# A hybrid decoder layer: attention and the down projection tied to the written instruction order, and four PSUM banks swapped in the second half

## The chip, the cores and the metric

The kernel runs on one core of one Trainium2 chip. The core has a matrix engine (TensorE, PE in the profile, with its weight loads as PEld), three engines for elementwise work (VectorE: DVE, ScalarE: ACT, GpSimd: POOL) and SyncE (SP), which issues all DMAs of this kernel. Each engine works through a list of instructions of its own, in the order of that list, and engines wait for each other through semaphores. The metric is the device time of one execution in microseconds (us).

## The reference

One layer of a decoder trunk over 2048 positions and 1024 channels, in float32. Two parts of it matter here, the forgetting attention (8 heads of 64) and the last product of the channel MLP:

```python
def forgetting_attention(q, k, v, f_pre):
    F = jnp.cumsum(jax.nn.log_sigmoid(f_pre.astype(jnp.float32)), axis=-1)
...
        logits = (jnp.einsum('bhtd,bhsd->bhts', qb, kb).astype(jnp.float32) * scale
                  + F[:, :, lo:hi, None] - F[:, :, None, :hi])
...
        p = jax.nn.softmax(logits, axis=-1)
        outs.append(jnp.einsum('bhts,bhsd->bhtd', p.astype(v.dtype), vb))

def conv_ffn(h, w_up, w_conv, b_conv, w_down):
...
    return (jax.nn.silu(a) * gv) @ w_down
```

Around them stand a norm, one combined input projection, an mLSTM and a gating unit, the output projection, the up projection and a causal convolution.

## The kernel before

The kernel is written with a tile framework. The program text names, for each instruction, its engine and its tiles; the framework allots buffers, sets the semaphores, and, with its scheduling turned on (line 1797), puts the instructions of each engine into an order of its own, from a simulated timeline. So the order in which the code writes two independent instructions of an engine is not the order in which the chip runs them.

The stages follow each other: projections and mLSTM, attention, output projection, up projection with convolution, down projection. Products of two float32 operands are made of three TensorE products of "hi" and "lo" halves (mm3, lines 53 to 56): ScalarE makes the hi half by a cast, VectorE the lo half by a subtraction.

**Attention** (lines 190 to 290). For each head h there are four blocks tb of 512 queries, each of four rows of 128 queries. `scores` handles a row in one or two parts of up to 1024 keys: TensorE makes the scores in a double-bank PSUM tile `sp` (two of them; lines 206 and 210), VectorE adds the bias, stores the tile L and keeps the row's extreme (line 212). For tb 0 and 1 a row has one part, of 128 to 512 and of 640 to 1024 keys; for tb 2 and 3 a part of 1024 keys and a second part of 128 to 512 and of 640 to 1024. `exps` (line 220) then makes a row's exponentials on ScalarE, one instruction for a part (line 223), and GpSimd scales L by the row's sum (lines 225 to 228). `exps` is called when the generator is resumed for the following part, so in the written order it stands just ahead of the next part's scores. `finish` takes a finished block in units j of 128 keys: up to four transposes on TensorE into a PSUM tile `tp` (three of them; line 259), a cast on ScalarE (262), a subtraction on VectorE (263), and, three units later, two products with the values (245 and 246) into the one bank `op`, which ScalarE copies out at the end of a block (250). `phase` (line 269) writes the two streams into one: the scores of one block with the units of the block before it. After part n of n_sc it writes units until (n + 1)(n_fin - 5) / n_sc are done, n_fin being 4, 8, 12 or 16 for a block tb of 0 to 3; the last five units, and all four of tb 0, stand behind the last part. While attention runs, `load_w` (line 309) also loads and splits the weights of the output projection.

**Down projection** (class Down, lines 486 to 636). The product of the activations with w_down is made by a seven-product scheme (Winograd's form of Strassen's), for each half H of the positions: products p in the order 1, 2, 7, 6, 5, 4, 3, each in 11 steps k of 12 matmuls, four banks at a time. `load` starts a step's DMAs five steps ahead. `prep` makes a step's operands three steps ahead: sums on VectorE (lines 1523 to 1539; one for products 5, 4 and 3, two for product 7, three for product 6), then for two operands a cast on ScalarE (1544) and a subtraction on VectorE (1545), into 12 tiles `wsp`, four for a step. `mm` issues the step's matmuls. `post` queues the evictions of a finished product in the list `later`, from which three are written behind each step (lines 1764 to 1766), in the next product's first three steps: 12 VectorE instructions for products 2, 5 and 4, four for product 7, 16 for product 6, 8 for product 3, and four ScalarE copies for product 1. The main loop, lines 1714 to 1769, writes for each step the loads, the `prep` of three steps on, the `mm`, then the evictions.

PSUM has eight banks; the down projection uses them as two sets of four, db0 and db1. Line 1555 counts the products that take a new set, and products alternate between the sets; product 3 adds into the banks of product 5 and isn't counted. So the six new sets of one half leave the count even, and product 1 of the second half takes the set that product 3 of the first half has just filled.

## Time and profile before

| what | value |
|---|---|
| median of 3 runs | 2715.94 us (2714.63 to 2721.72) |
| time of the profiled execution | 2716.23 us |
| its span, first to last instruction | 2714.5 us |
| PE busy | 2588.1 us |
| PEld busy | 2132.3 us |
| DVE busy | 1997.7 us |
| ACT busy | 1268.5 us |
| POOL busy | 412.0 us |
| mean granted TensorE clock | 0.984 |

The span is divided about so: projections and mLSTM to 719 us, where the first scores run; attention to 1192 us; output projection; up projection to 2232 us; down projection to the end. A line of a group names the source line, the engine, the operation, output and inputs, their shape and count, then the busy time, the mean of one in ns, and the idle time of the engine ahead of it with what ended it. A line of the timeline has the start, the length, the instruction, a count where equal ones are merged, and in brackets the idle time before it.

### The profile page before, as it was taken

Reading aid. Unit: us, or ns where it says so; the run is one execution under the profiler, and the core shown is the slowest. Engines: PE = TensorE matmul, PEld = TensorE weight load, DVE = VectorE, ACT = ScalarE, POOL = GpSimd, SP = SyncE. Lnnn points to the kernel's source line nnn. Section 1 sums busy time; section 2 is a strip of 40 time slices with the busy share of each in tenths; the row PEclk is TensorE's granted clock in tenths of the full one; section 3 lists DMA queues with packets and bytes.
Section 4 is the critical chain, followed back from the end, with each engine's and each line's share of the span. In section 5 each row is a group of like instructions: output and inputs, shape, how many; then the busy total and the mean of one; then the engine's idle time right before and its main releaser. Section 6 shows DMA issues by size and latency. Waiting matters only on the chain.

```text
span 2714.5 us, 36970 instructions
## 1 busy us (share of the span) xinstructions
PE 2588.1 (95%) x12761; PEld 2132.3 (79%) x12761; DVE 1997.7 (74%) x3460; ACT 1268.5 (47%) x2425; POOL 412.0 (15%) x550
## 2 busy tenths in 40 slices
PE   6999999999989999989989999999999999899899
PEld 5887878888768787877868888888888887678677
DVE  7546556574478888846679888888888877887886
ACT  4323342332368878834455444444444444334333
POOL 4012210122246656610000000000000000000000
PEclk8999999999999999999999999999999999999999
DMA  7626454334554535147632222264222248266523
GB/s 245 184 79 183 136 169 142 98 98 125 167 156 111 143 105 175 48 142 250 252 93 78 86 87 84 86 239 141 81 82 86 79 139 302 81 217 225 182 74 113
DMA packets 297812, 377.52 MB, mean 139 GB/s; under 512 B 31246, under 2 KB 189804, under 8 KB 295576
## 3 DMA queue, kind: packets, MB, share of 16 engines
q1 hardware_dynamic: 297624, 375.16, 43.5%
q8 instruction: 100, 1.64, 0.3%
q14 instruction: 88, 0.72, 0.1%
HBM read 274.34 MB, written 100.74 MB: 138 GB/s over the span
## 4 chain that ended last, share of the span: by engine, by line
PE 64%; DVE 9%; DMA 8%; issue 2%; ACT 1%; POOL 1%; SPq 1%; DVEq 0%; ACTq 0%; POOLq 0%
PE ub L55 10%; PE ub L54 10%; PE ub L56 10%; PE sp L206 4%; PE tp L259 3%; PE db L55 3%; PE db L56 3%; PE db L54 3%; PE acc L54 3%; PE acc L56 2%; PE acc L55 2%; PE op L246 2%; PE op L245 2%; DVE wspl L1545 2%; DMA ld<-y_d 2%
## 5 line engine op out<-in xcount | busy, mean ns | idle before, releaser
L54 PE MATMUL acc<-wh,hh 128*128 128x512 f32 (+2 forms) x768 | 284.6, 373 | 1.8 <-DVE vhl L783 1.0
L55 PE MATMUL db<-wspl,wsph 128*128 128x512 f32 x616 | 247.8, 402 | 31.5 <-DVE wspl L1545 31.4
L55 PE MATMUL acc<-wl,hh 128*128 128x512 f32 (+2 forms) x768 | 275.6, 361 | 0.3 <-DVE wl L625 0.3
L54 PE MATMUL ub<-T,wsph 128*128 128x512 f32 x704 | 273.1, 390 | 2.4 <-ACT T L1239 2.1
L55 PE MATMUL ub<-T,wsph 128*128 128x512 f32 x704 | 274.2, 390 | 0.6 <-DVE T L1240 0.6
L56 PE MATMUL ub<-T,wspl 128*128 128x512 f32 x704 | 272.9, 389 | 0.0
L56 PE MATMUL acc<-wh,hl 128*128 128x512 f32 (+2 forms) x768 | 271.9, 361 | 0.4 <-DVE hl L595 0.4
L56 PE MATMUL db<-wsph,wspl 128*128 128x512 f32 x616 | 243.7, 396 | 0.0
L263 DVE TENSOR_TENSOR plo<-tp,phi 128x512 fp32r<-128x512 f32 (+1 forms) x320 | 188.6, 606 | 57.7 <-ACT phi L262 55.8
L54 PE MATMUL ub<-B,wsph 128*128 128x512 f32 x528 | 207.5, 393 | 8.0 <-ACT s L1440 4.0
L55 PE MATMUL ub<-B,wsph 128*128 128x512 f32 x528 | 207.3, 393 | 0.0
L56 PE MATMUL ub<-B,wspl 128*128 128x512 f32 x528 | 207.0, 392 | 0.0
L1413 ACT CAST wsph<-S 128x512 fp32r<-128x512 f32 x176 | 109.2, 622 | 200.5 <-PE ub L55 153.6
L262 ACT CAST phi<-tp 128x512 fp32r<-128x512 f32 (+1 forms) x320 | 161.5, 520 | 83.6 <-PE tp L259 81.3
L1544 ACT CAST wsph<-act 128x512 fp32r<-128x512 f32 x132 | 82.3, 623 | 222.1 <-PE db L55 211.8
L223 ACT ACTIVATE L<-L,nm 128x1024 f32<-128x1024 f32 (+2 forms) x192 | 172.7, 903 | 17.2 <-DVE nm L212 15.5
L259 PE MATMUL tp<-ident,L 128*128 128x128 f32 x1088 | 174.1, 277 | 4.9 <-DVE plo L263 2.9
L206 PE MATMUL sp<-kk,q 128*128 128x512 f32 (+3 forms) x640 | 163.4, 373 | 14.2 <-DVE nm L212 7.9
L55 PEld LDWEIGHTS db<-wspl,wsph 128*128 128x128 f32 x616 | 117.7, 191 | 70.4 <-DVE wspl L1545 46.3
L54 PE MATMUL db<-wsph 128*128 128x512 f32 x616 | 168.7, 393 | 3.1 <-ACT wsph L1544 2.6
L228 POOL TENSOR_SCALAR L<-L,rs 128x1024 f32<-128x1024 f32 (+2 forms) x192 | 166.4, 876 | 11.7
L54 PEld LDWEIGHTS acc<-wh,hh 128*128 128x128 f32 x768 | 146.5, 191 | 21.3 <-DVE vhl L783 1.1
(344 smaller groups left out, 6050.8 us busy)
## 6 DMA issues: line engine op xcount, KB each, us to landing
w<-in_w_up_dram SPq DMA_DIRECT2D x88, 512.0 KB
wd<-in_w_down_dram SPq DMA_DIRECT2D x176, 256.0 KB
wa<-in_w_ada_dram SPq DMA_DIRECT2D x96, 256.0 KB
act_d<-yc SPq DMA_DIRECT2D x44, 512.0 KB
act<-act_d SPq DMA_DIRECT2D x44, 512.0 KB
wr<-in_w_in_dram SPq DMA_DIRECT2D x68, 256.0 KB
q<-q_d SPq DMA_DIRECT2D x128, 128.0 KB
hc_d<-hl SPq DMA_DIRECT2D x28, 512.0 KB
```

Of the source, the lines that this page charges most:

```text
L54: T.matmul(ps, lh, rh, start=start, stop=False, skip_group_check=resume)
L55: T.matmul(ps, lh, rl, start=False, stop=False, skip_group_check=resume)
L56: T.matmul(ps, ll, rh, start=False, stop=stop, skip_group_check=resume)
L206: T.matmul(sp[:, b : b + bw], q2[n][:, qs], kk[:, s0 + b : s0 + b + bw], start=n == 0, stop=n == 1 and not last)
L223: A.activation(L[c], L[c], AF.Exp, bias=nm[:, n - 1 : n], scale=-1.0, accum_out=rs[:, c : c + 1])
L228: G.tensor_scalar(t, t, rs[:, 0:1], 1.0, op0=ALU.mult, op1=ALU.mult)
L245: T.matmul(op[:, c0:], vv[:, j, :], hi[:, c0:], start=(j == 0), stop=False)
L259: T.transpose(tp[:, i * P : (i + 1) * P], rows[i][j // 8][:, (j % 8) * P : (j % 8 + 1) * P], ident)
L262: A.copy(hi[:, c0:], tp[:, c0:])
L263: V.tensor_tensor(lo[:, c0:], tp[:, c0:], hi[:, c0:].bitcast(F32), op=ALU.subtract)
L1413: A.copy(hi, src)
L1544: A.copy(hi, v)
```

## The change

`keep_in_program_order` takes an instruction and ties it behind the instruction that the code wrote just before it for the same engine: the scheduler may no longer move it ahead of that one. It sets the order of issue only and adds no wait for the end of the other. The change calls it O and wraps every TensorE, VectorE, ScalarE and GpSimd instruction of `scores`, `exps` and `finish`, and every VectorE and ScalarE instruction of Down. The matmuls of Down, all DMAs, and `load_split` stay free.

The second part moves one line: the count of bank sets goes up for product 3 too. Each half then counts seven, and the second half begins with the other set, so that its product 1 doesn't take the banks of the first half's product 3.

```diff
+    O = tc.keep_in_program_order
...
-                        T.matmul(
+                        O(T.matmul(
                             sp[:, b : b + bw], q2[n][:, qs], kk[:, s0 + b : s0 + b + bw], start=n == 0, stop=n == 1 and not last
-                        )
+                        ))
...
-                V.tensor_tensor_reduce(
+                O(V.tensor_tensor_reduce(
...
-                    A.activation(L[c], L[c], AF.Exp, bias=nm[:, n - 1 : n], scale=-1.0, accum_out=rs[:, c : c + 1])
+                    O(A.activation(L[c], L[c], AF.Exp, bias=nm[:, n - 1 : n], scale=-1.0, accum_out=rs[:, c : c + 1]))
...
-                    G.tensor_scalar(t, t, rs[:, 0:1], 1.0, op0=ALU.mult, op1=ALU.mult)
+                    O(G.tensor_scalar(t, t, rs[:, 0:1], 1.0, op0=ALU.mult, op1=ALU.mult))
...
-            T.matmul(op[:, c0:], vv[:, j, :], hi[:, c0:], start=(j == 0), stop=False)
+            O(T.matmul(op[:, c0:], vv[:, j, :], hi[:, c0:], start=(j == 0), stop=False))
...
-            A.copy(hi[:, c0:], tp[:, c0:])
-            V.tensor_tensor(lo[:, c0:], tp[:, c0:], hi[:, c0:].bitcast(F32), op=ALU.subtract)
+            O(A.copy(hi[:, c0:], tp[:, c0:]))
+            O(V.tensor_tensor(lo[:, c0:], tp[:, c0:], hi[:, c0:].bitcast(F32), op=ALU.subtract))
...
-                A.copy(hi, v)
-                V.tensor_tensor(lo, v, hi.bitcast(F32), op=ALU.subtract)
+                O(A.copy(hi, v))
+                O(V.tensor_tensor(lo, v, hi.bitcast(F32), op=ALU.subtract))
...
             if k == 0:
+                n_bank[0] += 1
                 if more:
                     self.ps[3] = self.ps[5]
                 else:
-                    n_bank[0] += 1
```

The sums of `prep` and all evictions of Down (lines 1523 to 1539 and 1579 to 1635) are wrapped in the same way.

## The prediction

> **What bounds the kernel now.** I read the page first, then the windows by stage, then the timeline and the groups by form inside the two stages that the change touches.

> ```profile
> span 2714.5 us, 36970 instructions
> ...
> PE 2588.1 (95%) x12761; PEld 2132.3 (79%) x12761; DVE 1997.7 (74%) x3460; ACT 1268.5 (47%) x2425; POOL 412.0 (15%) x550
> ```

> ```profile
> core 0: us, PE busy (x) PEld busy (x) DVE busy (x) ACT busy (x) POOL busy (x), PEclk, DMA share, GB/s
> ...
> 914.23:965.75 51.52, 49.40 (x313) 41.10 (x313) 43.68 (x89) 42.60 (x93) 30.97 (x48) 1.00 0.42 124
> ...
> 2300.10:2380.90 80.80, 67.88 (x265) 51.97 (x265) 69.68 (x115) 25.13 (x45) 0.00 (x0) 0.94 0.32 108
> 2380.90:2477.10 96.20, 92.16 (x397) 73.53 (x395) 80.00 (x132) 38.24 (x68) 0.00 (x0) 1.00 0.73 254
> ...
> 2537.30:2617.20 79.90, 65.42 (x266) 49.55 (x265) 69.97 (x116) 25.12 (x45) 0.00 (x0) 0.98 0.29 97
> 2617.20:2707.80 90.60, 90.54 (x397) 73.96 (x395) 71.65 (x118) 35.36 (x62) 0.00 (x0) 1.00 0.35 116
> ```

> The page says TensorE. By stage it is less plain. The first window is one whole head of attention: 51.52 us, with TensorE, VectorE and ScalarE all at 83% or more. The other four are the down projection, for each half products 7 and 6, then 5, 4 and 3. In 7 and 6 TensorE is idle by some 13 us.

> What a head costs TensorE alone comes from the distance of starts:

> ```profile
> 939.31 0.60 PE L259 MATMUL tp<-ident,L 128*128 128x128 f32 x4
> ...
> 940.21 0.60 PE L259 MATMUL tp<-ident,L 128*128 128x128 f32 x4
> ...
> 941.12 0.60 PE L259 MATMUL tp<-ident,L 128*128 128x128 f32 x4
> ```

> ```profile
> 2496.29 1.07 PE L54 MATMUL db<-wsph 128*128 128x512 f32 x4
> ...
> 2499.01 1.07 PE L54 MATMUL db<-wsph 128*128 128x512 f32 x4
> ```

> A full unit (four transposes, two products) takes 0.905 us. A step of Down, 12 matmuls, takes 2.72 us, so one of 512 columns takes 0.227. A head has 136 blocks of 128 by 128: 34 full units' worth, 30.8 us; scores, two matmuls for each block, 136 x 2 x 0.227 / 4 = 15.4; 16 masks of about 0.07, 1.1. In all 47.3 us. So the scheduler's order loses 51.5 - 47.3 = 4.2 us a head, and no order can win more there.

> **Attention: what the written order does.** In the written order ScalarE gets for each row of tb 3: both exponentials of the row, the cast of the unit behind the next row's first part, the cast of the unit behind its second part, then the next pair. VectorE gets: reduction of part one, subtraction, reduction of part two, subtraction. That closes a circle: the exponentials of row i need its second reduction; the next cast queues behind them on ScalarE; its subtraction needs the cast; row i + 1's second reduction queues behind that subtraction on VectorE; and the next exponentials need that reduction. The same collision stands once in the trace, where two exponentials happen to be ahead of casts:

> ```profile
> 934.71 1.15 ACT L223 ACTIVATE L<-L,nm 128x1024 f32<-128x1024 f32 x1
> ...
> 935.86 1.14 ACT L223 ACTIVATE L<-L,nm 128x1024 f32<-128x1024 f32 x1
> ...
> 936.99 1.54 ACT L262 CAST phi<-tp 128x512 fp32r<-128x512 f32 x3
> ```

> ```profile
> 937.59 1.89 DVE L263 TENSOR_TENSOR plo<-tp,phi 128x512 fp32r<-128x512 f32 x3 [2.69 <-ACT phi L262]
> ```

> ```profile
> 937.61 0.50 PE L245 MATMUL op<-phi,vv 128*128 128x512 f32 x1 [1.11 <-ACT phi L262]
> ```

> VectorE stood 2.69 us and TensorE 1.11. The scheduler has moved most units to stretches without long exponentials, such as 939 to 942 above. The written order can't. The circle's prices:

> ```profile
> L223 ACT ACTIVATE L<-L,nm 128x1024 f32<-128x1024 f32 x68 | 78.5, 1156 | 3.4 <-DVE nm L212 2.3
> ...
> L262 ACT CAST phi<-tp 128x512 fp32r<-128x512 f32 x190 | 107.7, 585 | 41.2 <-PE tp L259 40.6 <-DVE plo L263 0.2
> L223 ACT ACTIVATE L<-L,nm 128x896 f32<-128x896 f32 x12 | 12.5, 1040 | 0.0
> ...
> L223 ACT ACTIVATE L<-L,nm 128x768 f32<-128x768 f32 x13 | 12.2, 939 | 0.0
> L223 ACT ACTIVATE L<-L,nm 128x640 f32<-128x640 f32 x13 | 10.8, 830 | 0.0
> ...
> L223 ACT ACTIVATE L<-L,nm 128x512 f32<-128x512 f32 x13 | 9.3, 717 | 1.6 <-DVE nm L212 1.6
> ```

> ```profile
> L212 DVE CUSTOM_DVE_ANT_0 L<-sp,nf 128x1024 f32<-128x1024 f32 x60 | 73.3, 1222 | 5.8 <-PE sp L206 4.1 <-PE tp L259 0.3
> ...
> L212 DVE CUSTOM_DVE_ANT_0 L<-sp,nf,nm 128x1024 f32<-128x1024 f32 x7 | 8.9, 1274 | 0.0
> L212 DVE CUSTOM_DVE_ANT_0 L<-sp,nf,nm 128x896 f32<-128x896 f32 x7 | 8.0, 1143 | 0.1
> L212 DVE CUSTOM_DVE_ANT_0 L<-sp,nf,nm 128x768 f32<-128x768 f32 x7 | 7.1, 1008 | 0.0
> ...
> L212 DVE CUSTOM_DVE_ANT_0 L<-sp,nf,nm 128x640 f32<-128x640 f32 x7 | 6.1, 874 | 0.0
> ```

> ```profile
> L263 DVE TENSOR_TENSOR plo<-tp,phi 128x512 fp32r<-128x512 f32 x224 | 150.1, 686 | 44.5 <-ACT phi L262 43.1
> ```

> One turn is: exponential of 1024, exponential of the row's width, cast, subtraction, next row's second reduction. For tb 3: 1.156 + 0.830 + 0.585 + 0.686 + 1.008 = 4.27; 1.156 + 0.939 + 0.585 + 0.686 + 1.143 = 4.51; 1.156 + 1.040 + 0.585 + 0.686 + 1.274 = 4.74; together 13.5 us. Ahead of them stand the first row's scores (four matmuls and the last one's end, about 1.1), 1.222 and 0.874, 3.2; behind them the last exponentials, a cast and a subtraction, 2 x 1.156 + 0.585 + 0.686 = 3.6, and about one and a half units of TensorE, 1.3, since three tp tiles let only three units go ahead. Sum 21.6 us. TensorE's own work in this phase is 58 blocks of scores (6.6), masks (0.3) and 42 blocks of units (9.5): 16.4.

> The other phases in the same way, TensorE's work first:
> - tb 2: 42 blocks of scores and 26 of units, 11.0. Five of its eight units stand behind the last exponentials: wait 1.156 + 0.717 + 0.585 + 0.686 = 3.1. Of its turns one has a unit in it; I estimate 1.0. 15.1 us.
> - tb 1: 5.5; its four units wait for the last exponential, a cast and a subtraction, 1.156 + 0.585 + 0.686 = 2.4, and the copy of `op` (a cast's length) 0.6: 8.5 us.
> - tb 0: 14.5; the copy of `op`: 15.1 us.

> A head: 15.1 + 8.5 + 15.1 + 21.6 = 60.3 us, against 51.5: 8.8 us more. I count heads 1 to 6, 53 us. Head 0 begins under the projections; in head 7 the output projection's products, which stay free, can fill TensorE's waits: nothing, up to 15 us more. The lower bound is what the order could do without a circle, 47.3: 4.2 less a head. I take the circle, because each link is a true dependence or a place in a queue that the change fixes. Bank limits add nothing that the scheduler's order hasn't too.

> The weights of the output projection, split between rows of head 6, stay free; but the next tied instruction stands behind the last of these splits. Cover is the idle time that the circle makes. Without it I allow 15 us, in the upper end.

> **Down projection.** VectorE's instructions of 512 columns start 0.60 us apart:

> ```profile
> 2476.30 2.48 DVE L1623 TENSOR_TENSOR o<-db,gt 128x512 f32<-128x512 f32 x4
> 2478.70 0.68 DVE L1545 TENSOR_TENSOR wspl<-act,wsph 128x512 fp32r<-128x512 f32 x1
> ```

> ```profile
> PE db L55 <- DVE wspl L1545: 31.4, 26, 2.9
> ```

> Products 7 and 6 are 22 steps, 59.8 us of TensorE; the windows are 80.8 and 79.9, losses of 21.0 and 20.1. VectorE did 115 and 116 instructions in them, 69 us of work: it bounds them, and stood for some 10 us besides, partly behind sums hoisted ahead of their DMAs:

> ```profile
>   DMA wd<-in_w_down_dram: 17.2, 14
> ```

> The written order has nearly as many there (eight steps of 7 by four, eleven of 6 by five, three of 5 by three, evictions 12 and 4: 112), but none far ahead of its turn: it loses 69 - 60 = 9.4 us. It pays later: the evictions of products 6, 5 and 4 are written into three steps each. In product 5 these steps hold 9 + 16 = 25 instructions, 15.0 us against 8.2, less a reserve of 2.9 (two steps less one preparation): 3.9. In 4 and 3, 21 instructions each, 12.6 - 8.2 - 2.9 = 1.5. A half loses 9.4 + 3.9 + 1.5 + 1.5 = 16.3, both 32.6. Before, with 33 steps being 89.8 us, it was 21.0 + 6.4 + 20.1 + 0.8 = 48.3. The gain would be 15.7; I take off 3 for subtractions that wait for casts in the strict order: 12.7, between 0 and 20.

> **The banks.** The wait removed:

> ```profile
> 2477.13 0.47 PE L54 MATMUL db<-wsph 128*128 128x512 f32 x1 [0.39 <-DVE o L1623]
> ```

> It is 0.4 us. [...] Without the swap the written order would stop for good: the second half's preparation, ahead of product 3's evictions on VectorE, would wait for a matmul that waits for these evictions. So the swap is a need more than a gain.

> **The sum.** Against the profiled execution's own 2716.23 us (0.3 us off the median): 53 for attention, -12.7 for Down, -0.4 for the banks, and 6 for the clock, between nothing and 37, as follows.

> ```profile
> 2300.00:2360.00 60.00, 47.08 (x174) 34.80 (x173) 59.30 (x99) 17.12 (x30) 0.00 (x0) 0.91 0.39 132
> ```

> With TensorE busy for 78% of a stretch its granted clock was 0.91; 47.3 of 60.3 is 78% too. At 0.91 a head's 47.3 us would take 4.7 longer, eight heads 37; but the lost clock falls largely on waits, so I take 6. [...] Sum 2716.2 + 53 - 12.7 - 0.4 + 6 = 2762.

> **Rivals.**
> 1. Faster: the written order pipelines as it reads, and attention goes at TensorE's pace, 47.3 plus about 1 a head. It needs the turns of 4.3 to 4.7 us to fall to TensorE's work in a row of tb 3, (16.4 - 5 x 0.905) / 4 = 3.0; that is, casts not queueing behind exponentials. Then 7 x -3.2 - 13 = -35: 2681. For it: 4.2 us a head are there. Against it: the 2.69 us shown. Chance 0.13.
> 2. Same: ties to one neighbour change little and the scheduler's order survives in effect: 2716 less or more 8. Against it: units stand at 939 to 942 far from their written places. Chance 0.03.
> 3. Slower still: the clock falls to 0.91 in all of attention and hits work, not waits: 2762 + 31 = 2793. For it the row above; against it 1.00 in the head shown. Chance 0.08.
> 4. The forecast, 0.76.

> **Range.** Low: half of the circle's cost, full gain in Down, no clock: 2716 + 27 - 20 = 2723. High: 2762 + 15 for the weights and head 0, + 25 of clock: 2802. A measurement of this kernel tells about 0.3%, 8 us, from no change. Faster 0.13, same 0.03, slower 0.84 (the forecast and rival 3).

> **What would show it.** After: distance between heads about 60 us; VectorE's idle time before L263, ended by the cast of L262, far above 44.5 us in its group; exponentials in pairs on ScalarE with TensorE waiting behind L263; TensorE's wait for L1545 in Down below 31.4 and none on L1525's DMA; no wait of the second half's first matmul for L1623. Heads at 49 us or less would prove the circle wrong; heads at 51 would prove that the order wasn't changed.

## The result, and the profile after

The changed kernel takes 2813.99 us (median of 4 runs, 2807.05 to 2816.68) against 2717.95 (median of 4), a ratio of 1.0353 with a 95% interval of 1.0336 to 1.0370: 96 us slower. The forecast had the sign, but 46 us, and a range that ended at 2802.

The page of the changed kernel, first the span, then the busy time of each engine:

```profile
span 2812.0 us, 36827 instructions
...
PE 2626.5 (93%) x12746; PEld 2148.2 (76%) x12761; DVE 2016.3 (72%) x3460; ACT 1275.9 (45%) x2425; POOL 414.6 (15%) x550
```

Attention as one window, from the first scores to the last product with the values. Columns: window and length, busy time of the five engine rows with instructions in brackets, granted clock, DMA share, GB/s. Before:

```profile
719.10:1191.70 472.60, 445.30 (x2665) 365.02 (x2663) 363.25 (x729) 352.03 (x760) 253.26 (x388) 0.99 0.42 120
```

After:

```profile
722.20:1289.10 566.90, 481.25 (x2658) 376.19 (x2658) 370.78 (x729) 356.06 (x761) 253.56 (x388) 0.94 0.36 100
```

Attention is 94.3 us longer. The first column after the length divides that: TensorE stood 566.90 - 481.25 = 85.7 us instead of 27.3, 58 more; and its busy time for the same work is 36 us longer, at a granted clock of 0.94 instead of 0.99. Before attention the first scores start 3.1 us later, at 722.2; in the traces of the other kernels below they start anywhere between 714 and 723, so it can't be put down to the change. From attention's end to Down there is no difference. Down itself takes 482.3 and 482.4 us, from 2232.2 and from 2329.65 to the end of the span. Its two heavy parts of each half, in the windows that the prediction used for before:

```profile
2395.20:2467.90 72.70, 65.08 (x265) 49.75 (x264) 68.81 (x110) 25.94 (x43) 0.00 (x0) 0.98 0.42 136
2467.90:2569.28 101.38, 93.19 (x397) 75.03 (x396) 88.00 (x140) 38.62 (x68) 0.00 (x0) 0.98 0.64 229
2629.12:2701.89 72.77, 64.70 (x265) 49.85 (x264) 68.89 (x110) 25.94 (x43) 0.00 (x0) 0.98 0.41 136
2701.89:2804.94 103.05, 93.21 (x397) 74.81 (x395) 86.88 (x138) 36.51 (x63) 0.00 (x0) 0.98 0.32 105
```

Products 7 and 6 (first and third line) fell from 80.8 and 79.9 us to 72.7 and 72.8; products 5, 4 and 3 (second and fourth) rose from 96.2 and 90.6 to 101.4 and 103.1. What is won in one place is paid in the next.

One head of attention after, by its blocks tb 0, 1, 2 and 3, and as a whole:

```profile
989.90:1005.85 15.95, 15.37 (x104) 12.94 (x102) 11.63 (x23) 11.24 (x25) 4.33 (x8) 0.98 0.30 99
1005.85:1014.87 9.02, 6.75 (x39) 5.31 (x38) 6.17 (x13) 6.21 (x13) 5.79 (x8) 0.98 0.32 89
1014.87:1031.67 16.80, 13.62 (x72) 10.29 (x70) 10.97 (x23) 10.92 (x25) 9.36 (x17) 0.91 0.39 110
1031.67:1054.73 23.06, 19.25 (x103) 14.38 (x102) 15.99 (x30) 14.77 (x29) 11.40 (x17) 0.94 0.39 96
989.90:1054.73 64.83, 54.98 (x313) 42.93 (x312) 44.76 (x88) 43.14 (x92) 30.88 (x48) 0.95 0.36 99
```

The forecast had 15.1, 8.5, 15.1 and 21.6. In block 3 of this head the first exponentials of the four rows start here, with the links of the first turn between them (start, length, instruction, idle time before it and what ended it):

```profile
1035.15 1.15 ACT L225 ACTIVATE L<-L,nm 128x1024 f32<-128x1024 f32 x1 [0.63 <-DVE nm L214]
...
1037.12 1.05 ACT L264 CAST phi<-tp 128x512 fp32r<-128x512 f32 x2
...
1037.71 0.69 DVE L265 TENSOR_TENSOR plo<-tp,phi 128x512 fp32r<-128x512 f32 x1 [0.91 <-ACT phi L264]
...
1038.32 1.01 DVE L214 CUSTOM_DVE_ANT_0 L<-sp,nf,nm 128x768 f32<-128x768 f32 x1
...
1039.43 1.15 ACT L225 ACTIVATE L<-L,nm 128x1024 f32<-128x1024 f32 x1 [0.78 <-POOL L L230]
...
1043.95 1.16 ACT L225 ACTIVATE L<-L,nm 128x1024 f32<-128x1024 f32 x1 [1.41 <-DVE nm L214]
...
1048.70 1.15 ACT L225 ACTIVATE L<-L,nm 128x1024 f32<-128x1024 f32 x1 [1.53 <-DVE nm L214]
```

The turns are 4.28, 4.52 and 4.75 us; worked out were 4.27, 4.51 and 4.74. The circle exists. In its first turn the two exponentials take 1.97 us up to the start of the cast, the cast 0.59 up to the subtraction, the subtraction 0.61 up to the reduction, and the reduction 1.11 up to the next exponential; the prices were 1.99, 0.59, 0.69 and 1.01. So the links are right, and the agreement to 0.01 us is in part luck, since the last two differences cancel. (For the second row the profile names GpSimd's scaling as what came last; the read of the reduction ended 0.10 us before that exponential too.) VectorE's wait for the casts is the one that was announced, 101.2 us in place of 43.1:

```profile
L265 DVE TENSOR_TENSOR plo<-tp,phi 128x512 fp32r<-128x512 f32 x224 | 152.3, 688 | 102.3 <-ACT phi L264 101.2
```

Behind the last of these exponentials TensorE looks like this:

```profile
1049.27 0.55 PE L261 MATMUL tp<-ident,L 128*128 128x128 f32 x3 [0.68 <-DVE plo L265]
1049.57 0.48 PE L247 MATMUL op<-phi,vv 128*128 128x512 f32 x1
...
1052.33 0.69 PE L261 MATMUL tp<-ident,L 128*128 128x128 f32 x2 [2.04 <-DVE plo L265]
1052.67 0.77 PE L247 MATMUL op<-phi,vv 128*128 128x512 f32 x1
```

TensorE waits 2.04 us for a tile `tp` whose subtraction (L265) waits for a cast behind two exponentials. The same product of 512 columns takes 0.48 us before that wait and 0.77 after it, since the clock has gone down (the last two lines are the 3.41 us around the wait and the 3.41 us behind them):

```profile
1048.00:1052.00 4.00, 1.61 (x9) 0.74 (x7) 1.63 (x4) 3.29 (x7) 2.07 (x4) 1.00 0.93 238
1052.00:1056.00 4.00, 3.67 (x16) 3.18 (x17) 2.35 (x7) 1.12 (x5) 2.21 (x2) 0.57 0.99 291
...
1048.59:1052.00 3.41, 1.02 (x6) 0.58 (x5) 1.04 (x4) 3.29 (x7) 1.48 (x3) 1.00 0.98 239
1052.00:1055.41 3.41, 3.08 (x12) 2.59 (x13) 2.05 (x5) 1.05 (x4) 2.21 (x2) 0.50 0.98 269
```

So a phase's end is paid twice, in waits and in slow matmuls behind them.

### The profile page after: what moved, and what is told of

It is laid out like the page before. It is cut to its first block, busy times and chain, and to the rows that moved or that the text cites. A ratio compares the mean times of both kernels' runs of the same rounds, so it can differ in the third digit from the quotient of the medians.

```text
span 2812.0 us, 36827 instructions
## 1 busy us (share of the span) xinstructions
PE 2626.5 (93%) x12746; PEld 2148.2 (76%) x12761; DVE 2016.3 (72%) x3460; ACT 1275.9 (45%) x2425; POOL 414.6 (15%) x550
## 4 chain that ended last, share of the span: by engine, by line
PE 56%; DVE 12%; ACT 6%; DMA 5%; issue 5%; POOL 0%; SPq 0%; ACTq 0%; DVEq 0%; POOLq 0%
PE ub L54 10%; PE ub L55 10%; PE ub L56 10%; PE sp L208 3%; PE acc L54 3%; DVE wspl L1547 3%; PE acc L56 3%; PE acc L55 3%; PE tp L261 2%; ACT L L225 2%; PE db L54 2%; PE db L55 2%; ACT wsph L1546 2%; PE db L56 2%; DVE L L214 2%
## 5 line engine op out<-in xcount | busy, mean ns | idle before, releaser
L54 PE MATMUL acc<-wh,hh 128*128 128x512 f32 (+2 forms) x768 | 284.6, 373 | 1.6 <-DVE vhl L785 0.7
L54 PE MATMUL ub<-T,wsph 128*128 128x512 f32 x704 | 273.5, 390 | 2.9 <-ACT T L1241 2.2
L55 PE MATMUL acc<-wl,hh 128*128 128x512 f32 (+2 forms) x768 | 275.6, 361 | 0.0
L55 PE MATMUL ub<-T,wsph 128*128 128x512 f32 x704 | 274.8, 391 | 0.6 <-DVE T L1242 0.6
L265 DVE TENSOR_TENSOR plo<-tp,phi 128x512 fp32r<-128x512 f32 (+1 forms) x320 | 188.8, 608 | 116.3 <-ACT phi L264 113.9
L55 PE MATMUL db<-wspl,wsph 128*128 128x512 f32 x616 | 242.8, 394 | 0.0
L261 PE MATMUL tp<-ident,L 128*128 128x128 f32 x1088 | 180.7, 283 | 49.1 <-DVE plo L265 49.1
L54 PE MATMUL ub<-B,wsph 128*128 128x512 f32 x528 | 207.5, 393 | 8.0 <-ACT s L1442 4.0
L55 PE MATMUL ub<-B,wsph 128*128 128x512 f32 x528 | 207.1, 392 | 0.0
L54 PE MATMUL db<-wsph 128*128 128x512 f32 x616 | 172.1, 400 | 36.4 <-ACT wsph L1546 36.2
L261 PEld LDWEIGHTS tp<-ident,L 128*128 128x128 f32 x1088 | 131.4, 145 | 87.2 <-DVE plo L265 65.5
L208 PE MATMUL sp<-kk,q 128*128 128x512 f32 (+3 forms) x640 | 172.6, 395 | 22.3 <-DVE nm L214 13.4
L54 PEld LDWEIGHTS db<-wsph 128*128 128x128 f32 x616 | 113.5, 189 | 73.4 <-ACT wsph L1546 51.5
L230 POOL TENSOR_SCALAR L<-L,rs 128x1024 f32<-128x1024 f32 (+2 forms) x192 | 166.3, 875 | 12.6
L214 DVE CUSTOM_DVE_ANT_0 L<-sp,nf 128x1024 f32<-128x1024 f32 (+7 forms) x128 | 126.0, 986 | 58.8 <-PE sp L208 35.2
```

Source lines behind the costliest of these rows:

```text
L54: T.matmul(ps, lh, rh, start=start, stop=False, skip_group_check=resume)
L55: T.matmul(ps, lh, rl, start=False, stop=False, skip_group_check=resume)
L208: O(T.matmul(sp[:, b : b + bw], q2[n][:, qs], kk[:, s0 + b : s0 + b + bw], start=n == 0, stop=n == 1 and not last))
L214: O(V.tensor_tensor_reduce(out=L[c], in0=sp[:, :w], in1=nf[:, s0 : s0 + w], scale=-1.0, scalar=3.0e38 if c == 0 else nm[:, 0:1], op0=ALU.a ...
L230: O(G.tensor_scalar(t, t, rs[:, 0:1], 1.0, op0=ALU.mult, op1=ALU.mult))
L261: O(T.transpose(tp[:, i * P : (i + 1) * P], rows[i][j // 8][:, (j % 8) * P : (j % 8 + 1) * P], ident))
```

## The experiments

Sixteen kernels, all compared with the kernel before. "Tied" means that the change's ties are in place. In the five traces below in which attention is as before it takes 475 to 477 us, a little more than the 472.6 above.

| kernel | us | ratio to before, 95% interval | attention, us | TensorE busy in it | clock in it |
|---|---|---|---|---|---|
| attention tied only | 2809.09 | 1.0344 [1.0323, 1.0365] | 567.5 | 481.2 | 0.94 |
| Down tied only, banks swapped | 2721.76 | 1.0022 [1.0008, 1.0035] | | | |
| banks swapped only | 2716.46 | 1.0005 [0.9992, 1.0017] | | | |
| Down tied, one item a step | 2713.24 | 0.9984 [0.9972, 0.9997] | | | |
| TensorE tied only | 2755.50 | 1.0140 [1.0122, 1.0159] | 517.9 | 454.1 | 0.98 |
| VectorE, ScalarE, GpSimd tied only | 2793.04 | 1.0279 [1.0260, 1.0299] | 551.9 | 481.6 | 0.95 |
| attention tied, exponentials split | 2781.11 | 1.0235 [1.0213, 1.0257] | 535.4 | 466.9 | 0.96 |
| attention tied, late subtraction | 2779.51 | 1.0225 [1.0205, 1.0246] | 532.3 | 463.8 | 0.96 |
| attention tied, units carried over | 2727.06 | 1.0048 [1.0033, 1.0064] | 484.3 | 445.3 | 0.98 |
| the last three together | 2718.43 | 1.0009 [0.9996, 1.0022] | 476.3 | 447.8 | 0.98 |
| Down tied, one item, late subtraction | 2685.69 | 0.9892 [0.9875, 0.9909] | | | |
| Down tied, late subtraction | 2701.99 | 0.9948 [0.9928, 0.9967] | | | |
| attention tied, tail of two units | 2809.16 | 1.0338 [1.0322, 1.0353] | 569.6 | 480.2 | 0.92 |
| TensorE tied, units carried over | 2722.63 | 1.0021 [1.0008, 1.0033] | 482.1 | 442.5 | 0.98 |
| all edits, all ties | 2685.19 | 0.9880 [0.9865, 0.9894] | | | |
| all edits, attention's ties off | 2685.24 | 0.9872 [0.9855, 0.9890] | | | |

**The parts of the change alone.** Each kernel keeps one part: the ties in `scores`, `exps` and `finish`; or those in Down with the banks; or the banks alone.

```diff
-    O = tc.keep_in_program_order
+    O = tc.keep_in_program_order; I = lambda ins: ins
...
-                O(A.copy(hi, v))
+                I(A.copy(hi, v))
```

> Attention is tied, Down and its banks are as before. Read from the two traces, from the first scores to the last product with the values: 472.6 us before, 567.1 after, so 94 us more; the down projection 482.3 in both. If that division is the whole story: 2716 + 94 = 2810 (2804 to 2816). If attention's ties only cost by what they do together with Down's (its loads or its splits started earlier or later): well under 2800.

> Down is tied and has the banks swapped, attention is as before. By the trace of after, where the losses of products 7 and 6 fall by 15 us and those of products 5, 4 and 3 rise by 17: 2716, within 5. By the forecast's sizes, if the loss in after came from attention's delay (other DMAs at that time): 2703.

> Nothing is tied; only the second half of Down starts in the other banks. The wait before its first matmul was 0.39 us in the trace of before: 2715.5, no difference. The rival: the scheduler lays out another order around the swapped banks, and that moves up to 10 us either way.

Attention alone is the whole loss, 2809. Down alone costs 5 us, less than the 8 that count as a difference here; the gain that the forecast gave it does not come in either kernel. The banks do nothing by themselves.

**Which engine's order.** Ties are left on TensorE's calls alone, or on all but TensorE's; Down is as before.

> In attention only TensorE's instructions are tied; VectorE, ScalarE and GpSimd are free, Down is as before. If the circle of VectorE and ScalarE sets the loss: the scheduler can put casts ahead of exponentials, and most of the 94 us goes away, 2710 to 2745. If TensorE's written order itself loses (units evenly dealt, five behind the last exponentials, no scores of the next block ahead of them): 2780 to 2815.

> In attention VectorE's, ScalarE's and GpSimd's instructions are tied, TensorE's are free; Down is as before. If the circle sets the loss: nearly all of it stays, 2790 to 2815. If TensorE's written order loses: 2716 to 2745.

TensorE's order alone costs 40 us, the other engines' 77, both together 93. The two share a part. The first kernel lies in neither of its ranges. The second lies in the range that was given for the circle, but the runs below show that this range could not tell the circle from the ends of the phases.

**Breaking the circle, in two ways.** In the first the second exponential of a row is written one part later, so that a cast stands between the two. In the second a unit's subtraction is written one unit later.

```diff
             for c, (s0, w) in enumerate(parts):
+                if c == 1 and held:
+                    held.pop()()
...
-            exps()
+            exps((0,))
+            if len(parts) == 2:
+                held.append(lambda exps=exps: exps((1,)))
```

```diff
-            O(V.tensor_tensor(lo[:, c0:], tp[:, c0:], hi[:, c0:].bitcast(F32), op=ALU.subtract))
+            if held:
+                held.pop()()
+            held.append(lambda lo=lo, hi=hi, tp=tp, c0=c0: O(
+                V.tensor_tensor(lo[:, c0:], tp[:, c0:], hi[:, c0:].bitcast(F32), op=ALU.subtract)
+            ))
+            if j == ns - 1:
+                held.pop()()
```

> Attention is tied on all engines as in after, Down is as before; but the second exponential of a row of two parts is written one part later, so that on ScalarE a cast stands between the two. By the circle one turn loses an exponential: in block 3 the turns of 4.28, 4.52 and 4.75 us (after) fall to VectorE's own work of a row, 1.22 + 1.01 to 1.27 + 2 x 0.69 and the small reads, 3.8 to 4.0; with a share of it in block 2, 2 to 4 us a head, 2810 - 16 to 32 = 2778 to 2794. If the circle isn't what sets the turn: 2805 to 2815.

> Attention is tied as in after, Down is as before; but the subtraction of a unit is written one unit later, behind VectorE's next reduction, so that this reduction no longer stands behind a cast. By the circle the turns in block 3 fall to VectorE's own work, 3.8 to 4.0, and 2 to 4 us a head are won: 2778 to 2794. If the circle isn't what sets the turn: 2805 to 2815, or slower, since a unit's transposes and products wait longer.

Both give what the circle said, 28 and 30 us. With the late subtraction the four rows of block 3 start so:

```profile
1016.68 1.15 ACT L225 ACTIVATE L<-L,nm 128x1024 f32<-128x1024 f32 x1 [0.63 <-DVE nm L214]
...
1020.06 1.17 ACT L225 ACTIVATE L<-L,nm 128x1024 f32<-128x1024 f32 x1
...
1023.14 1.15 ACT L225 ACTIVATE L<-L,nm 128x1024 f32<-128x1024 f32 x1
...
1026.99 1.15 ACT L225 ACTIVATE L<-L,nm 128x1024 f32<-128x1024 f32 x1 [0.30 <-DVE nm L214]
```

Turns of 3.38, 3.08 and 3.85 us in place of 4.28, 4.52 and 4.75: 3.2 us a head. Two of them are shorter than the 3.8 to 4.0 that I expected. But two thirds of the loss stay.

**The ends of the phases.** Next, the five units that stand behind a block's last part are written in the next phase.

```diff
-        fin = (u for t in then for u in finish(*t))
+        units = (u for t in then for u in finish(*t))
+        old, n_old = carried.pop() if carried else ((), 0)
+        fin = (u for g in (old, units) for u in g)
+        n_fin += n_old
...
-        for _ in fin:
-            pass
+        if now and hold:
+            carried.append((fin, n_fin - done))
+        else:
+            for _ in fin:
+                pass
```

> Attention is tied on all engines as in after, Down is as before; but the five units (four for a block with four) that stand behind a block's last part are written in the next phase, dealt among its parts, so that TensorE gets the next block's scores ahead of them. In after TensorE waits in a head 2.1, 0.9, 1.6, 0.7 and 2.0 us, 7.3 in all, in these tails behind the last exponentials. If the ends of the phases are the part of the loss that the circle leaves (they are TensorE's own order, as its 40 us alone say): heads of 64.8 fall to 58 to 60, 2809 - 7 x 5 to 7 = 2760 to 2775. If the waits only move into the next phase: 2795 to 2815.

> As the kernel that carries the last units over, and with the two edits that break the circle as well (second exponential one part later, subtraction one unit later). If circle and ends are two separate parts of the loss: about 30 us less than with the carrying alone, 2725 to 2745, heads near 54. If they are the same waits counted twice: no better than the better of the single edits by more than 10 us.

Carrying wins 82 us, far more than I expected; with the circle broken too, 91, which is the time of the kernel before. The carrying kernel's turns in block 3, and one head:

```profile
984.57 1.16 ACT L225 ACTIVATE L<-L,nm 128x1024 f32<-128x1024 f32 x1 [0.76 <-DVE nm L214]
...
988.38 1.16 ACT L225 ACTIVATE L<-L,nm 128x1024 f32<-128x1024 f32 x1 [0.83 <-DVE nm L214]
...
992.90 1.16 ACT L225 ACTIVATE L<-L,nm 128x1024 f32<-128x1024 f32 x1 [0.42 <-DVE nm L214]
...
997.94 1.16 ACT L225 ACTIVATE L<-L,nm 128x1024 f32<-128x1024 f32 x1 [0.38 <-DVE nm L214]
```

```profile
944.70:997.20 52.50, 49.77 (x313) 40.87 (x312) 43.67 (x89) 42.92 (x93) 31.14 (x49) 1.00 0.42 121
```

The turns are 3.81, 4.52 and 5.04 us, 13.4 together as in the changed kernel (13.5), yet the head takes 52.5 us and not 64.8. The turns were never what cost most: between the turns TensorE has work. What carrying removes is most of the stop at each block's end: in this head TensorE stands for 2.7 us in place of 9.9, and the clock is back at 1.00.

Two readings were left, so I tried a shorter tail without carrying, and carrying with TensorE's ties alone:

```diff
-            while done < (n + 1 - lead) * (n_fin - 5) // (n_sc - lead):
+            while done < (n + 1 - lead) * max(0, n_fin - 2) // (n_sc - lead):
```

> Attention is tied on all engines, Down is as before, nothing is carried over; but a block's phase deals out all but two of the units among its own parts, where it was all but five. Two readings of the 82 us that the carrying won: (a) the phases' ends, where TensorE has neither the next block's scores nor operands behind the last exponentials; then a shorter tail saves only what stands behind the last exponentials, about 1.4 in each of the three larger phases, 4 a head, 2809 - 28 = 2780 (2770 to 2800). (b) too few units under the circle's turns, which the carrying raised from about 0.9 to 1.5 a part in block 3; then most of it comes here too, 2730 to 2750.

> Only TensorE is tied in attention, Down is as before, and the last units are carried into the next phase. If the 40 us of TensorE's ties alone are the ends of the phases: 2755 falls to 2715 to 2730. If they are something else in TensorE's written order: 2745 to 2755.

The shorter tail wins nothing, against both readings. TensorE's waits in attention are 89.4 us with it, against 86.3 in the kernel with attention tied only. The clock is lower too, 0.92 in 569.6 us of attention where the changed kernel has 0.94 in 566.9: 45.6 us are lost to it and not 34.0, so some 12 us of a gain may be hidden there (an estimate that counts all of them as work). More units under the turns do not shorten the waits by themselves; and a tail that is shorter only moves the wait into the next phase, where the first unit of the new block now stands for the last row's scaling on GpSimd:

```profile
1029.98 0.47 PE L261 MATMUL tp<-ident,L 128*128 128x128 f32 x1 [2.79 <-POOL L L230]
```

That is the chain of a block's end: last reduction, two exponentials, scaling, first unit of this block. As I read it, something must cover it: the next block's scores, and the old units, whose casts must not stand behind those exponentials while nothing else is open to TensorE. Carrying gives both, a shorter tail neither. No run shows which of the two counts more. With TensorE's ties alone carrying takes 40 us down to 6, so nearly all of these 40 were the ends too.

**Down.** One eviction item behind each step in place of three; the subtractions one step later; both.

```diff
-        for _ in range(1 if s[0] == "up" else 3):
+        for _ in range(1 if s[0] == "up" else 1):
```

```diff
+            if held_d:
+                held_d.pop(0)()
+            halves, subs = [], []
...
-                O(V.tensor_tensor(lo, v, hi.bitcast(F32), op=ALU.subtract))
+                subs.append(lambda lo=lo, v=v, hi=hi: O(V.tensor_tensor(lo, v, hi.bitcast(F32), op=ALU.subtract)))
...
+            held_d.append(lambda: [f() for f in subs])
```

> As the kernel with Down alone tied, but one eviction item is written behind each step of Down in place of three. If the stalls of products 5, 4 and 3 (11.6 and 13.3 us a half in after) are VectorE's bursts: at one item a step VectorE has at most five instructions of 0.61 us in a step, 3.05 against 2.72, for eight steps, which the reserve of 2.9 us hides; the stalls fall to 0 to 3 a half, and the time to 2694 (2690 to 2700). If they come from banks that are free too late or from DMAs, later evictions make it no better, 2716 or more.

> As the kernel with Down alone tied, three items a step, with only the subtractions one step later. This takes the waits for casts out of the forecast's sum for Down, which counted instructions: 9.4 + 3.9 + 1.5 + 1.5 = 16.3 a half against the 26 of that kernel. If these waits are what the forecast mis-sized: 2722 - 2 x 9.7 = 2702 (2698 to 2708). If the bursts are larger than counted: 2715 to 2722.

> Attention is free as before. Down is tied with one eviction item a step, and a step's two subtractions are written one step later, behind the next step's sums, so that VectorE has no cast to wait for. The rival to the first theory of Down's bursts, read from the run with one item a step: a sum that starts at 0 is followed by its subtraction at 1.44 at the earliest (sum, cast, subtraction), so steps with five instructions take 3.36 to 3.98 us and not 3.05. If this chain is it: product 7 loses 2, product 6 7, products 5 to 3 about 3 a half, 12 against 21.8, and the time is 2713 - 20 = 2693. If VectorE's count of instructions is all: 2710 to 2716.

The first is a miss: 8.5 us less than with three items, where 22 were expected (2694 in place of 2716). Its trace in product 3 shows why (VectorE and ScalarE, one step):

```profile
2677.50 0.68 DVE L1541 TENSOR_TENSOR act<-act 128x512 f32<-128x512 f32 x1
2678.29 0.62 ACT L1546 CAST wsph<-act 128x512 fp32r<-128x512 f32 x1 [2.12 <-DVE act L1541]
...
2678.95 0.69 DVE L1547 TENSOR_TENSOR wspl<-act,wsph 128x512 fp32r<-128x512 f32 x1 [0.76 <-ACT wsph L1546]
...
2679.55 0.69 DVE L1547 TENSOR_TENSOR wspl<-wd,wsph 128x512 fp32r<-128x512 f32 x1
2680.16 0.69 DVE L1581 TENSOR_TENSOR o<-db,u 128x512 f32<-128x512 f32 x1
```

A sum starts at 2677.50, its cast 0.79 later, its subtraction 1.45 after the sum. In the written order nothing lies between sum and subtraction, so VectorE stands for 0.76 us in this step, with the next step's sum queued behind. With the subtractions one step later the kernel lands on the 2702 that counting instructions alone gives, and with one item a step as well on 2686.

**All together.**

> All that helped at once, with all ties of the change and its banks: in attention the carrying, the split exponentials and the late subtraction; in Down one eviction item a step and the late subtractions. If the two stages add up: 2718 - 31 = 2687 (2680 to 2695), below both kernels. If attention's speed comes back as Down's loss: 2700 or more.

> The same text as the kernel with all that helped, with attention's ties taken off and Down's kept. If the scheduler goes its own way whatever is written: as the one with attention as before, 2686 (2680 to 2692). If it leans on the written order where its timeline leaves a choice: 2665 to 2680, or worse than 2692.

The gains add up: this version is 1.2% faster than the kernel before, 31 us. With attention's ties off the time is the same: the scheduler's own order and a mended written order are worth the same in attention, and all of the gain over the kernel before is Down's: the kernel with Down's edits alone takes 2686 too.

## Why the prediction was wrong

- **The sign and the place** were right: attention is the whole loss, and the circle turned at the lengths that were worked out. The heads did not: heads 1 to 6 grew by 81 us in all, not 53; head 0 grew by 12.8, and head 7 by 0.7.
- **The clock** is the first term that was mis-sized, by some 14 us. The step that failed is "the lost clock falls largely on waits", which put 6 us beside an upper bound of 37. No run shows that step, nor the "nothing" at which the term's range begins: the clock of attention is 0.94 after and was 0.99 before. In the traces of before and after the granted clock is 1 or 0.5, and its 35 and 51 changes lie whole numbers of 3.41 us apart. In attention TensorE was busy at half clock for 12.9 us before, of 13.7 at half clock, and for 56.1 after, of 68.3. So it fell on work. By the prediction's spacings (0.227 us for 512 columns, a unit of 0.905) the work done in these 56.1 us is worth 27.9 at full clock, and that in the 12.9 us before 6.8. Products of 512 columns start 0.43 us apart at half clock (after, from 2445.66 on) and 0.227 at full, a factor of 1.9. By that the clock makes some 20 of the 36 us by which TensorE's busy time grew; counted at a factor of two it is half of 56.1 - 12.9, 21.6 (estimates). The rival "slower still" had this mechanism, with a chance of 0.08. In the head above no long pause stood ahead of it: TensorE's longest wait there was 2.1 us, and from 1048.59 to 1052.00 it was busy for 1.02 us of 3.41, and the clock was 0.50 in the next 3.41.
- **What went ahead of a lower clock** can be read from the attention of two traces, before and after. Cut at the places where the clock can be seen to change, every 3.41 us, it holds 278 whole stretches at full clock. Each of the 14 that TensorE filled to between 0.24 and 0.39 was followed by half clock, of the five from 0.44 to 0.52 it was three, and of the 259 from 0.57 up none. (In the rest of these two executions it was all 19 up to 0.39, five of 13 from 0.44 to 0.53, and three of 1221 above, filled to 0.55, 0.62 and 0.76.) So in this attention one thin stretch was enough, and the waits' sum does not say how many there are: with TensorE's ties alone it waits for 64 us in attention, and the clock there is 0.98; after, it waits for 86, the clock falls 14 times, against 3 before, and is 0.94.
- **A term that the sum does not have** is TensorE's busy time at full clock, by these estimates at least 14 of the 36 us. Four products of 512 columns in a row take 1.07 us (before, at 2496.29), and the record of a single one 0.39; so I estimate that work that is broken by waits takes longer, and in attention TensorE stood for more than 0.05 us at 103 places after and at 41 before. With TensorE's ties alone its busy time is 454.1 us, and 442.5 with units carried over, at a clock of 0.98 in both. That broken rows make up the whole rest is argued, not shown.
- **Down's gain**, 12.7 us, did not come. The step that failed is "I take off 3 for subtractions that wait for casts in the strict order". A half was to lose 16.3 us; it lost 12.9 in products 7 and 6 (counted: 9.4), 11.6 and 13.3 in 5 to 3 (counted: 6.9), 24.5 and 26.2 in all. (The 9.4 takes the work of 115 instructions; the 112 counted, at 0.60 us, would give 7.4.) TensorE no longer waits for subtractions there, 31.4 us before, but for casts, 36.2. The kernel with late subtractions differs in their place alone and is 20 us faster than the one without: the off-take should have been about 20, not 3.
- **TensorE's waits** were forecast at 53 us, from 8.8 a head in six heads, and grew by 58. The sum is close, but it hides an error: 47 of the 58 lie in heads 1 to 6, and head 0, which was counted at nothing, lost as much as the others (73.1 us between its first scores and head 1's, against 60.3).
- **The reason named** was incomplete. The forecast took the circle for the loss, and its "ends", 8.1 of the 21.6 us of block 3 and most of what was added in blocks 1 and 2, for additions to it. Breaking the circle wins 30 us, opening the ends 82, both 91. The ends are the larger part, and with them open most of the circle hides under TensorE's work. With the elementwise engines tied the ends come with the low clock, 0.94 and 0.95 in all of attention; with the units carried over it is 0.98. With TensorE alone tied it is 0.98 with the ends too.
- **The banks** were right: no time. That the written order needs the swap was argued; no run ties Down without it.
- **The weights of the output projection**: heads 5 and 6, where they are split, grew by 17.2 and 9.0 us, 13.1 in the mean, like the others (13.3 to 14.7 for heads 1 to 4). The 15 us allowed for them did not appear.

The sum of the two profiled executions: 3.1 ahead of attention, 58.4 of waits, 36.0 of longer busy time, 0.1 in Down: 97.6 against 97.5 between the spans. Of the 51 us that the forecast lacks, some 30 are TensorE's longer busy time (36 against 6), 13 are Down's, 5 the waits' and 3 the start of attention.

What stays open is how the 36 us divide between the clock, by estimate 20 to 21.6, and broken rows of matmuls. No kernel here changed the clock without the waits; the nearest thing is TensorE tied alone, which has longer waits than before at nearly the same clock and 9 us more of busy time.

## What to carry to other kernels

Tying an engine's stream to the written order makes that order the schedule; before doing so, read it queue by queue, above all at the ends of phases, where a chain of several engines (here reduction, exponentials, scaling, transposes) needs other independent work written around it. A subtraction written directly behind the cast that it needs stopped VectorE until the cast was done, for 0.76 us in the step shown; one step of delay in the text won 20 to 28 us of Down. When waits grow, look how they are spread: here the lower clock, 0.5 behind each of the 14 stretches of 3.41 us that they left filled to 0.39 or less, fell on the work that followed, not on the waits themselves.
